# Query and key weights of differential attention, heads 2 to 7: their two float parts made during the gated MLP ahead and read back from DRAM scratch

## The chip, the cores and the metric

The kernel runs on one core of a Trainium2 chip. The metric is the time of one execution on the device in microseconds (us), lower is better. A core has five engines that run their own instruction streams and wait for one another by semaphores: PE (TensorE, matrix products), DVE (VectorE), ACT (ScalarE), POOL (GpSimd) and SP (SyncE, which here only issues DMAs). Matrix products write PSUM; all other tiles lie in SBUF; weights and scratch lie in DRAM.

## The reference, cut to what matters

A first block (a pooling mixer and block-sparse attention under a gate, then an MLP with squared ReLU) is followed by a second block whose first layer is differential attention. Sequence 512, width 1024, float32 throughout. The parts that the change touches:

```python
        u2 = rmsnorm(h, norm_mlp_pre[l])
        a = jnp.square(jax.nn.relu(u2 @ w_up[l]))          # 1024 -> 4096
        h = h + rmsnorm(a @ w_down[l], norm_mlp_post[l])   # 4096 -> 1024
...
    q, k, v = jnp.split(h @ w_qkv, 3, axis=-1)             # 1024 -> 3 x 1024
    q = apply_rope(q.reshape(B, S, 2 * H, d), cos, sin)    # H = 8, d = 64
    k = apply_rope(k.reshape(B, S, 2 * H, d), cos, sin)
    v = v.reshape(B, S, H, 2 * d)
...
        s = jnp.einsum('bqhd,bkhd->bhqk', qb, k) * scale
        pr = jax.nn.softmax(s, axis=-1).reshape(B, H, 2, DIFF_Q_BLOCK, S)
        a = (pr[:, :, 0] - lam_full * pr[:, :, 1]).astype(v.dtype)
        return jnp.einsum('bhqk,bkhe->bqhe', a, v)
...
    o = rms_norm(o, subln) * (1.0 - lam_init)
    return o.reshape(B, S, H * 2 * d) @ w_o
```

"Gated MLP" is the name of the change's own words for the MLP of the first block (`w_up`, `w_down`), the stage right ahead of differential attention.

## The kernel before, in words

Every float32 product is made of three products of rounded parts. `split` and `w_split` write a tile as hi (the rounded copy, on ACT, for every third weight tile on POOL) and lo (source minus hi, on DVE); `mm3` (L102 to L107) then issues three matmuls: hi·hi (L105), hi·lo of the activations (L106), lo·hi (L107). A weight column block of 128 outputs is a tile of 128 partitions x 1024 values (8 slices of the contraction), so its product is 8 x 3 = 24 matmuls of 512 columns.

Weights come to SBUF in tiles `wst` of 128 x 2048 values (two column blocks, 1 MB, two buffers), loaded by SP (`stage`, L99, or in `tiles`, L116, as two loads of 512 KB where the two blocks are not adjacent: query and key of one head). `w_split` makes `whi` and `wlo` of each block, four buffers each. So weights run ahead of PE by up to three split blocks and two loaded tiles.

The MLP (in `block1`) has four groups g of 8 up columns (L751 on) and 8 down columns. An up column is evacuated by DVE (`t`, L754), squared and split by ACT and DVE (L756, L79, L80); a down column is added to `y` by DVE (L778). The first three columns of each down linear are computed together (`first=3`), the rest one by one.

Differential attention (`diff`) weaves two generators. `lin` computes the linears: queries and keys of a head (`qk`), values of two heads (`vv`), in the order qk 0 and 1 together, values 0, values 1, qk 2, qk 3, qk 4, values 2, qk 5, qk 6, values 3, qk 7, then `w_o`. Each query or key goes through `rope` (copy `rx` by ACT L807, four swap DMAs `rs` on SP L811, multiplications by POOL L812 and DVE L813 and L814, split) and is then stacked by three or more DMAs on SP (`stack_q`, `stack_k`, L836 to L845). `att` walks 8 heads x 4 query tiles t: `scores` (four matmuls `sc` L852; row maximum `st` on DVE L958; exponential `pr` on ACT L961; DVE L963 to L966), two tiles later `flip` (transposes `tr` L978, split into `Th` and `Tl`), then `values` (`pv`), and the norm of a finished head. Two PSUM banks hold scores; a bank is free when ACT has read it.

The order of each engine's stream is not written out by hand: `weave` gives a program order by estimated costs, and a list scheduler places each instruction where its own clock has it ready. On the chip each engine, SP too, takes its instructions strictly in that order.

## Time and profile before

| what | value |
|---|---|
| time before, median of 3 runs | 2002.96 us (2002.18 to 2003.5) |
| time of the profiled execution | 2004.46 us |
| its span, first to last instruction | 2002.7 us |
| PE busy | 1960.4 us (98%) |
| DVE busy | 1262.8 us (63%) |
| ACT busy | 800.7 us (40%) |
| POOL busy | 444.7 us (22%) |
| DMA queue of SP | 218.19 MB, 36.8% of 16 DMA engines |

The profiled execution is 1.5 us above the median of the runs. Engine, time and wait stand in each row of the trace; an engine's gap is put down to the instruction that ended it. PE's busy time is a modelled one of pipelined matmuls, so the gaps between its instructions tell more than its share.

### The profile page before, as it was taken

To read this page: it belongs to the slowest core of one execution; us is meant where nothing else is said; L and a number is where in the kernel's file an instruction comes from. 1 tells how busy PE (TensorE), PEld (TensorE's weight loads), DVE (VectorE), ACT (ScalarE), POOL (GpSimd) and SP (SyncE) were. 2 spreads that over 40 slices of the span, in tenths; PEclk is the share of its full clock that TensorE was granted. 3 is DMA by queue.
4 is the path that set the end of the run, shared out by engine and by line. 5 is a ranking of instruction groups with operands and counts; after the bars stand their busy time and mean duration, and the time that the engine had idled before them with its cause. 6 is when DMAs were issued, how large, how long until landed. Compare 5 with 4: busy or idle time off the path is not lost.

```text
span 2002.7 us, 25458 instructions
## 1 busy us (share of the span) xinstructions
PE 1960.4 (98%) x9400; PEld 1626.0 (81%) x9400; DVE 1262.8 (63%) x2087; ACT 800.7 (40%) x1392; POOL 444.7 (22%) x545
## 2 busy tenths in 40 slices
PE   8999999999999999999999999999998999999997
PEld 7797788788888887887788888887877788888886
DVE  6447755435444478897683565658797684565665
ACT  4325434322213345554342331335575342342342
POOL 4115421000000211110221123122343221113122
PEclk9999999999999999999999999999999999999999
DMA  6263543233332446443332333336522333334231
GB/s 195 85 163 85 153 133 120 97 106 102 103 106 87 142 148 160 128 121 93 106 105 89 102 105 85 90 121 181 134 79 82 85 106 105 94 96 143 79 105 63
DMA packets 263853, 224.33 MB, mean 112 GB/s; under 512 B 9957, under 2 KB 236338, under 8 KB 263730
## 3 DMA queue, kind: packets, MB, share of 16 engines
q1 hardware_dynamic: 260538, 218.19, 36.8%
q10 hardware_dynamic: 3192, 4.52, 0.7%
q8 instruction: 74, 1.21, 0.3%
q14 instruction: 49, 0.40, 0.1%
HBM read 182.83 MB, written 14.16 MB: 98 GB/s over the span
## 4 chain that ended last, share of the span: by engine, by line
PE 50%; DVE 7%; ACT 2%; issue 2%; DMA 1%; SPq 0%; POOL 0%; DVEq 0%; ACTq 0%; POOLq 0%
PE mm L105 7%; PE mm L107 7%; PE mm L106 7%; PE sc L107 6%; PE sc L105 6%; PE sc L106 6%; PE pv L105 3%; PE pv L106 3%; PE pv L107 3%; PE sc L852 1%; DVE wlo L94 1%; PE pv L861 1%; DVE st L958 1%; DVE Tl L80 1%; DVE pr L966 1%
## 5 line engine op out<-in xcount | busy, mean ns | idle before, releaser
L94 DVE TENSOR_TENSOR wlo<-wst,whi 128x1024 fp32r<-128x1024 f32 (+2 forms) x304 | 393.6, 1298 | 198.9 <-ACT whi L93 141.0
L93 ACT ACTIVATE whi<-wst 128x1024 fp32r<-128x1024 f32 (+2 forms) x203 | 207.2, 1026 | 435.0 <-PE sc L106 171.2
L105 PE MATMUL mm<-uh,whi 128*128 128x512 f32 x712 | 281.8, 396 | 0.6 <-DVE t L754 0.6
L106 PE MATMUL mm<-ul,whi 128*128 128x512 f32 x712 | 279.3, 392 | 1.1 <-DVE ul L83 1.1
L107 PE MATMUL mm<-uh,wlo 128*128 128x512 f32 x712 | 279.1, 392 | 0.0
L91 POOL TENSOR_SCALAR whi<-wst 128x1024 fp32r<-128x1024 f32 (+2 forms) x101 | 110.6, 1095 | 756.6 <-PE mm L106 268.5
L105 PE MATMUL sc<-uh,whi 128*128 128x512 f32 x488 | 191.2, 392 | 0.0
L106 PE MATMUL sc<-ul,whi 128*128 128x512 f32 x488 | 190.7, 391 | 0.2 <-DVE ul L83 0.2
L107 PE MATMUL sc<-uh,wlo 128*128 128x512 f32 x488 | 190.7, 391 | 0.0
L107 PEld LDWEIGHTS mm<-uh,wlo 128*128 128x128 f32 x712 | 134.3, 189 | 27.4
L106 PEld LDWEIGHTS mm<-ul,whi 128*128 128x128 f32 x712 | 134.4, 189 | 26.8 <-DVE ul L83 1.6
L105 PEld LDWEIGHTS mm<-uh,whi 128*128 128x128 f32 x712 | 134.5, 189 | 26.4 <-DVE t L754 0.8
L107 PEld LDWEIGHTS sc<-uh,wlo 128*128 128x128 f32 x488 | 91.9, 188 | 20.2 <-DVE wlo L94 0.7
L106 PEld LDWEIGHTS sc<-ul,whi 128*128 128x128 f32 x488 | 91.9, 188 | 19.1 <-DVE ul L83 0.5
L105 PEld LDWEIGHTS sc<-uh,whi 128*128 128x128 f32 x488 | 91.9, 188 | 18.7
L105 PE MATMUL sc<-ah,whi 128*128 128x512 f32 x264 | 102.8, 389 | 0.0
L107 PE MATMUL sc<-ah,wlo 128*128 128x512 f32 x264 | 102.7, 389 | 0.0
L106 PE MATMUL sc<-al,whi 128*128 128x512 f32 x264 | 102.7, 389 | 0.0
L105 PE MATMUL pv<-uh,whi 128*128 128x512 f32 x256 | 100.4, 392 | 1.0 <-DVE psl L83 1.0
L107 PE MATMUL pv<-uh,wlo 128*128 128x512 f32 x256 | 99.8, 390 | 0.0
L106 PE MATMUL pv<-ul,whi 128*128 128x512 f32 x256 | 99.8, 390 | 0.0
L1263 ACT ACTIVATE cv<-cu,cc 128x512 f32<-128x512 f32 x88 | 70.9, 813 | 60.2 <-DVE cu L1261 59.3
(460 smaller groups left out, 4307.4 us busy)
## 6 DMA issues: line engine op xcount, KB each, us to landing
wst<-ffn_w_up SPq DMA_DIRECT2D x88, 512.0 KB
wst<-w_up SPq DMA_DIRECT2D x16, 1024.0 KB
wst<-w_down SPq DMA_DIRECT2D x16, 1024.0 KB
wst<-ffn_w_down SPq DMA_DIRECT2D x16, 1024.0 KB
wst<-w_in SPq DMA_DIRECT2D x16, 512.0 KB
wst<-w_in SPq DMA_DIRECT2D x8, 1024.0 KB
wst<-diff_w_qkv SPq DMA_DIRECT2D x16, 512.0 KB
wst<-ple_w_gate SPq DMA_DIRECT2D x8, 1024.0 KB
```

The source lines that it names most:

```text
L80: nc.vector.tensor_tensor(lo, src, f32(hi), op=OP.subtract)
L91: nc.gpsimd.tensor_scalar(hi, src, 1.0, 1.0, op0=OP.mult, op1=OP.mult)
L93: nc.scalar.activation(hi, src, AF.Copy)
L94: nc.vector.tensor_tensor(lo, src, f32(hi), op=OP.subtract)
L105: nc.tensor.matmul(ps, ah, bh, start=first, stop=False)
L106: nc.tensor.matmul(ps, ah, bl, start=False, stop=False)
L107: nc.tensor.matmul(ps, al, bh, start=False, stop=last)
L852: self.nc.tensor.matmul(ps, q[m][:, qs], k[2 * step + m][:, ks], start=step == 0, stop=last and step == 1)
L861: nc.tensor.matmul(*args, start=first and x == 0, stop=last and x == 1)
L958: nc.vector.reduce_max(st[:, m:m + 1], ps, axis=AX.X, negate=True)
L966: nc.vector.scalar_tensor_tensor(pr[0], pr[1], st[:, 6:7], pr[0], op0=OP.mult, op1=OP.add)
L1263: nc.scalar.activation(v, u[:, 1:S + 1], AF.Identity, bias=cc[:, 3, ft:ft + 1], scale=cc[:, 1, ft:ft + 1])
```

## The change

`presplit` is a generator that takes 24 jobs: head 2 to 7, query or key, lower or upper half of the contraction. A job loads a half block `xs` (128 x 512 values, 256 KB) on SP, makes hi on ACT and lo on DVE (both tiles are called `xh` in the rows), and stores both (2 x 256 KB) on SP into DRAM scratch `xd0h`, `xd0l` to `xd11h`, `xd11l`. All three SBUF tiles have one buffer. One job is asked for after each evacuated column: 8 down columns of g = 1, 8 up columns and 8 down columns of g = 2. Later, `split_load` reads a block's parts from the scratch straight into `whi` and `wlo` (2 x 512 KB on SP) for qk 2 to 7, in place of the load to `wst` and the split.

```diff
@@ -93,6 +94,43 @@
+    def presplit(self, w, jobs, P, bufs):
+        nc = self.nc
+        src = w.rearrange("(k p) n -> p k n", p=128)
+        done = None
+        for key, k0, kt, cols in jobs:
+            n = 128 // len(cols)
+            st = P.tile([128, kt, 128], F32, name="xs", tag="xs", bufs=bufs)
+            for i, c in enumerate(cols):
+                nc.sync.dma_start(st[:, :, i * n:(i + 1) * n], src[:, k0:k0 + kt, c:c + n])
+            pair = [P.tile([128, kt, 128], F32R, name="xh", tag=t, bufs=bufs) for t in ("xh", "xl")]
+            nc.scalar.activation(pair[0], st, AF.Copy)
+            nc.vector.tensor_tensor(pair[1], st, f32(pair[0]), op=OP.subtract)
+            if bufs == 1:
+                self.split_store(key, k0, pair)
+            else:
...
+            yield
...
+    def split_store(self, key, k0, pair):
+        if key not in self.pres:
+            self.pres[key] = [self.dr.tile([128, KT, 128], F32, name="xd%d%s" % (len(self.pres), "hl"[i]))
+                              for i in range(2)]
+        for d, t in zip(self.pres[key], pair):
+            self.nc.sync.dma_start(d[:, k0:k0 + t.shape[1], :], f32(t))
+
+    def split_load(self, key):
+        wt = [self.wp.tile([128, KT, 128], F32R, name=t, tag=t, bufs=4) for t in ("whi", "wlo")]
+        for t, d in zip(wt, self.pres[key]):
+            self.nc.sync.dma_start(f32(t), d)
+        return wt
@@ -121,14 +159,14 @@
-        src = self.tiles(w, k0, kt, cols[len(ahead):])
+        src = (self.split_load(key) for key in pres) if pres else self.tiles(w, k0, kt, cols[len(ahead):])
@@ -758,6 +796,8 @@
                     at.append((hi, lo))
+                    if g >= 2:
+                        next(X, None)
@@ -768,6 +808,11 @@
+                if g == 1:
+                    X = self.presplit(a["diff_w_qkv_2"][0],
+                                      [(("d", h, n), k0, 4, [1024 * n + h * 128]) for h in range(2, KT)
+                                       for n in range(2) for k0 in (0, 4)],
+                                      cv.enter_context(tc.tile_pool(name="pre", bufs=1)), 1)
@@ -776,6 +821,8 @@
+                    if g in (1, 2):
+                        next(X, None)
@@ -784,6 +831,8 @@
+            assert next(X, None) is None
+            cv.close()
@@ -935,7 +984,7 @@
                 return self.linear_steps(w, self.u, [h * 128, 1024 + h * 128], evac,
-                                         hold=("dqkfree", h - 2) if h >= 2 else None)
+                                         hold=("dqkfree", h - 2), pres=[("d", h, 0), ("d", h, 1)])
```

What the scheduler makes of it is seen at three places of the streams. (The changed kernel's line numbers are higher: its L108 and L127 are the jobs' loads and stores, L110 and L111 their hi and lo, L132 the loads from scratch; L137, L143 to L145, L901 and L1027 are L99, L105 to L107, L852 and L978 of before.)

The first is SP's stream in the MLP, from the first up tile of g = 2 on; `xs` is a job's half block, `xd` the scratch, `wst` the MLP's weights. Before, the weight loads stand there alone:

```order
L99 DMA wst<-w_up 128x8x256 x4
L99 DMA wst<-w_down 128x8x256 x4
L99 DMA wst<-w_up 128x8x256 x4
```

The changed kernel has:

```order
L137 DMA wst_4562<-w_up 128x8x256
L108 DMA xs_4338<-diff_w_qkv_2 128x4x128
L137 DMA wst_4572<-w_up 128x8x256
L127 DMA xd0h_4344<-xh_4340 128x512
L127 DMA xd0l_4345<-xh_4341 128x512
L108 DMA xs_4349<-diff_w_qkv_2 128x4x128
L127 DMA xd0h_4344<-xh_4351 128x512
L127 DMA xd0l_4345<-xh_4352 128x512
L108 DMA xs_4358<-diff_w_qkv_2 128x4x128
L137 DMA wst_4666<-w_up 128x8x256
L127 DMA xd1h_4364<-xh_4360 128x512
L127 DMA xd1l_4365<-xh_4361 128x512
```

Between two weight tiles there are now two jobs, six DMAs, and each weight load stands between a job's load and its stores.

The second is ACT's stream at the start of the down linear of g = 2 in the changed kernel; `s` and `ah` are of the last up column, `whi` the split of weight blocks. Of these rows the stream of before has only those on `s`, `ah` and `whi`, in the same order.

```order
L794 ACTIVATE s_4924<-t_4922 128x512
L80 ACTIVATE ah_4926<-s_4924 128x512
L110 ACTIVATE xh_4801<-xs_4799 128x512
L110 ACTIVATE xh_4848<-xs_4846 128x512
L110 ACTIVATE xh_4889<-xs_4887 128x512
L94 ACTIVATE whi_5066<-wst_5064 128x1024
L94 ACTIVATE whi_5070<-wst_5064 128x1024
```

Jobs 12, 13 and 14 (counted from 0) stand in front of the splits of two weight blocks.

The third is the begin of the scores in differential attention, on PE and on SP. Before, PE has finished the query of head 2 (`pv`, 24 matmuls) when the scores of head 0 (`sc`) begin, and goes on with its key (`mm`) between them:

```order
L106 MATMUL pv_6371<-ul7_5811,whi_6363 128x512
L107 MATMUL pv_6371<-uh7_5810,wlo_6364 128x512
L852 MATMUL sc_6398<-st2_6060,st0_6010 128x512
L852 MATMUL sc_6399<-st3_6061,st1_6011 128x512
L852 MATMUL sc_6398<-dl1_6062,st0_6010 128x512
L852 MATMUL sc_6399<-dm_6075,st1_6011 128x512
L105 MATMUL mm_6488<-uh0_5796,whi_6367 128x512
L106 MATMUL mm_6488<-ul0_5797,whi_6367 128x512
```

In the changed kernel the first two matmuls of head 2's query are followed by fourteen score matmuls and a flip (`tr`), of which the last rows are shown, and only then comes the first matmul that reads `wlo`:

```order
L1027 MATMUL tr_6664<-ident_72,pr0_6622 128x128 x4
L901 MATMUL sc_6648<-st3_6281,st1_6231 128x512
L901 MATMUL sc_6648<-dm_6295,st1_6231 128x512
L901 MATMUL sc_6672<-st2_6280,st0_6230 128x512
L901 MATMUL sc_6672<-dl1_6282,st0_6230 128x512
L145 MATMUL pv_6588<-uh0_6016,wlo_6581 128x512
L143 MATMUL pv_6588<-uh1_6018,whi_6580 128x512
```

On SP of the changed kernel the load of that `wlo` (`xd0l`) stands behind the stacking of heads 0 and 1 (`st`, `dm`, `dl`) and the swaps of head 1's key (`rs`), while that of its `whi` stands ahead of them:

```order
L132 DMA whi_6580<-xd0h_4344 128x1024
L892 DMA st3_6281<-st2_6280 64x512
L893 DMA st3_6281<-st2_6280 64x512
L892 DMA dm_6295<-dl1_6282 64x512
L893 DMA dm_6295<-dl1_6282 64x512
L885 DMA st5_6303<-st4_6302 64x512
L894 DMA st2_6280<-st2_6280 64x512
L886 DMA st5_6303<-dl0_6304 64x512
L894 DMA dl1_6282<-dl1_6282 64x512
L887 DMA st4_6302<-dl0_6304 64x512
L860 DMA rs_6325<-rx_6323 32x512 x4
L132 DMA wlo_6581<-xd0l_4345 128x1024
```

So the two parts of one weight block are now issued eleven rows apart, and the matmul that needs the second waits behind the scores of four query tiles.

## Rows read from the trace of the kernel before

**Rows 1.** The page: its span, and each engine's busy us, share of the span and instructions.

```profile
span 2002.7 us, 25458 instructions
PE 1960.4 (98%) x9400; PEld 1626.0 (81%) x9400; DVE 1262.8 (63%) x2087; ACT 800.7 (40%) x1392; POOL 444.7 (22%) x545
```

**Rows 2.** Busy time by stretch: the stretch in us, its length, busy us of PE, PEld, DVE, ACT, POOL (instructions), granted clock of PE (1.00 is 2.4 GHz), share of the DMA engines, GB/s. The first lies in the MLP, the second in differential attention.

```profile
540.00:590.00 50.00, 50.00 (x222) 41.42 (x221) 21.32 (x24) 11.44 (x15) 3.17 (x3) 1.00 0.33 105
750.00:800.00 50.00, 47.12 (x243) 38.30 (x242) 43.83 (x77) 28.47 (x59) 8.72 (x6) 1.00 0.63 159
```

**Rows 3.** Waits of PE from 740 to 955 us: who waited for whom, us in total, times, longest.

```profile
PE sc L852 <- ACT pr L961: 5.0, 6, 2.3
```

**Rows 4.** Groups of instructions from 740 to 960 us: line, engine, operation, tiles, shapes, count, then busy us and mean ns of one, then the idle time before them and its releasers.

```profile
L94 DVE TENSOR_TENSOR wlo<-wst,whi 128x1024 fp32r<-128x1024 f32 x23 | 30.2, 1312 | 6.3 <-ACT whi L93 3.8 <-POOL whi L91 2.4
L93 ACT ACTIVATE whi<-wst 128x1024 fp32r<-128x1024 f32 x16 | 16.8, 1058 | 5.8 <-PE mm L106 2.4 <-PE pv L107 1.8 <-PE sc L106 1.6
L961 ACT ACTIVATE pr<-sc,st 128x512 f32<-128x512 f32 x64 | 43.9, 690 | 27.9 <-DVE st L958 27.6
L961 ACT ACTIVATION_READ_ACCUMULATOR pr<-sc,st 128x1 f32 x64 | 12.7, 199 | 0.0
L958 DVE TENSOR_REDUCE st<-sc 128x1 f32<-128x512 f32 x64 | 43.1, 681 | 5.7 <-PE sc L852 5.7
```

**Rows 5.** Timeline of PE: start us, us, engine, line, operation, tiles, shapes, count, and in brackets the idle time before it and what ended it.

```profile
752.08 0.40 PE L105 MATMUL pv<-uh,whi 128*128 128x512 f32 x1
...
757.55 0.62 PE L852 MATMUL sc<-st,st 128*128 128x512 f32 x2
...
763.15 0.49 PE L852 MATMUL sc<-st,st 128*128 128x512 f32 x1 [0.23 <-ACT pr L961]
...
768.22 0.50 PE L852 MATMUL sc<-st,st 128*128 128x512 f32 x1 [2.26 <-ACT pr L961]
...
778.83 0.38 PE L106 MATMUL pv<-Tl,V 128*128 128x256 f32 x1 [0.39 <-DVE Tl L80]
...
803.36 0.50 PE L852 MATMUL sc<-st,st 128*128 128x512 f32 x1 [1.25 <-ACT pr L961]
```

**Rows 6.** Timelines of DVE and POOL ahead of the longest of these waits (768.22), columns as in rows 5.

```profile
763.70 2.31 DVE L94 TENSOR_TENSOR wlo<-wst,whi 128x1024 fp32r<-128x1024 f32 x1 [1.35 <-POOL whi L91]
766.67 0.68 DVE L958 TENSOR_REDUCE st<-sc 128x1 f32<-128x512 f32 x1
762.62 1.05 POOL L91 TENSOR_SCALAR whi<-wst 128x1024 fp32r<-128x1024 f32 x1 [1.66 <-DMA wst<-diff_w_qkv]
```

**Rows 7.** The chain of work that ended last: start us, us, what. The transfer is one of 512 KB, with four swaps of 64 KB issued beside it.

```profile
757.62 4.83 DMA wst<-diff_w_qkv
```

**Rows 8.** Timelines of POOL and SP around the rope of heads 0 and 1, columns as in rows 5; an SP row is a DMA's issue.

```profile
743.28 1.68 POOL L91 TENSOR_SCALAR whi<-wst 128x1024 fp32r<-128x1024 f32 x1 [6.10 <-ACT whi L93]
744.92 2.98 POOL L812 TENSOR_TENSOR rs<-rs,R 128x512 f32<-128x512 f32 x2
749.14 0.50 SPq L843 DMA_DIRECT2D st<-st  x1
757.62 0.58 SPq L116 DMA_DIRECT2D wst<-diff_w_qkv  x1
```

**Rows 9.** Timeline of DVE in the MLP: evacuations of two neighbouring up columns of g = 2, of its first down columns, the weight split ahead of the place of job 0, and a split of half a block's size.

```profile
497.45 1.21 DVE L94 TENSOR_TENSOR wlo<-wst,whi 128x1024 fp32r<-128x1024 f32 x1
522.00 0.69 DVE L754 SCALAR_TENSOR_TENSOR t<-mm,R 128x512 f32<-128x512 f32 x1 [3.35 <-PE mm L107]
524.06 0.69 DVE L80 TENSOR_TENSOR al<-s,ah 128x512 fp32r<-128x512 f32 x1
527.44 0.69 DVE L754 SCALAR_TENSOR_TENSOR t<-sc,R 128x512 f32<-128x512 f32 x1 [2.69 <-PE sc L107]
575.04 0.69 DVE L778 TENSOR_TENSOR y<-mm,y 128x512 f32<-128x512 f32 x1 [12.16 <-PE mm L107]
```

**Rows 10.** Timelines in the MLP: ACT's half-size split and its two weight splits at the start of the down linear of g = 2, and PE's first matmul with the block that they make.

```profile
561.47 0.63 ACT L79 ACTIVATE ah<-s 128x512 fp32r<-128x512 f32 x1
574.86 2.01 ACT L93 ACTIVATE whi<-wst 128x1024 fp32r<-128x1024 f32 x2 [12.76 <-PE mm L106]
581.64 0.39 PE L105 MATMUL pv<-ah,whi 128*128 128x512 f32 x1
```

**Rows 11.** Issues on SP in the MLP: two weight loads of 1 MB, one after the other.

```profile
507.80 0.37 SPq L99 DMA_DIRECT2D wst<-w_up  x1
518.73 0.37 SPq L99 DMA_DIRECT2D wst<-w_up  x1
```

**Rows 12.** A load of 1 MB by stretch, with no other transfer beside it (columns as in rows 2).

```profile
404.00:405.00 1.00, 1.00 (x6) 0.84 (x5) 0.98 (x1) 0.00 (x0) 0.00 (x0) 1.00 0.02 7
404.00:409.00 5.00, 5.00 (x24) 4.14 (x23) 2.20 (x2) 1.54 (x2) 0.00 (x0) 1.00 0.67 210
```

**Rows 13.** A store of 256 KB to DRAM scratch, issued by ACT, and the DVE instruction that waited for its landing (columns as in rows 5).

```profile
486.00 0.33 ACTq L288 DMA_DIRECT2D sin<-red  x1
488.14 1.34 DVE L283 SCALAR_TENSOR_TENSOR red<-kk,ang 128x512 f32<-128x512 f32 x1 [2.14 <-DMA sin<-red]
```

**Rows 14.** Two stretches in which PE was granted less than its full clock (columns as in rows 2).

```profile
365.00:370.00 5.00, 3.94 (x14) 2.95 (x14) 4.40 (x9) 4.16 (x7) 0.00 (x0) 0.77 0.51 163
370.00:375.00 5.00, 5.00 (x21) 4.04 (x21) 3.63 (x7) 3.19 (x6) 0.00 (x0) 0.89 0.00 0
```

More of the change, by code (lines that the diff above doesn't have):

```diff
@@ L48, in __init__ @@
         self.pjd = []
+        self.pres = {}
         self.consts()
@@ L95, in w_split @@
         return hi, lo
+    def presplit(self, w, jobs, P, bufs):
[13 more added lines that the diff above has]
+            else:
+                if done:
+                    self.split_store(*done)
+                done = key, k0, pair
+            yield
+        if done:
+            self.split_store(*done)
+    def split_store(self, key, k0, pair):
[9 more added lines that the diff above has]
+        return wt
     def stage(self, w, k0, kt, c0, nc_):
@@ L123, in linear_steps @@
     def linear_steps(self, w, x, cols, evac, k0=0, group=1, order=None, ready=None, first=None, ahead=(), hold=None,
-                     mid=None):
+                     mid=None, pres=None):
         kt = len(x)
```

## The prediction

> **What bounds the kernel now.** The page comes first: PE is busy 98% of the span and the next engine, DVE, 63% [rows 1]. So the kernel ends when PE has done its matmuls, and what a change of the other engines' work can give is no more than the time in which PE waits for them. The busy times by stretch say where that is: in the MLP PE is busy 50.00 of 50 us with DVE at 21 and ACT at 11, so there is room on both engines and nothing to gain; at the start of differential attention PE loses 2.9 of 50 us while DVE is busy 43.8 [rows 2]. There DVE is the near bound. The list of PE's waits names the chain: 5.0 us in six waits, scores that wait for the exponential that frees their PSUM bank [rows 3]; the timeline of PE adds 0.39 us for a split of transposed probabilities [rows 5]. These 5.4 us are all that the change can win in attention. Two of the waits stand close together at 763.15 and 768.22, 0.23 + 2.26 = 2.5 us [rows 5]. Their cause is one weight split: POOL's half of it waited for the load, DVE then waited 1.35 us for POOL and took 2.31 us, and the row maximum of the scores stood behind it until 766.67 [rows 6]. The load had taken 4.8 us [rows 7].
>
> **What is removed.** Twelve of the 23 weight splits of the attention stretch (six heads, query and key): on DVE 12 x 1.31 = 15.7 us of 200, and on ACT or POOL 12 copies of about 1.06 us [rows 4]. PE's matmuls stay. DVE's 43.8 of 50 us becomes about 40, so waits for its queue should shrink. The wait of 2.26 us is of the removed kind as to its cause, but its place is taken by another (below). Two more waits with row maxima or splits late in DVE's queue, 0.39 at 778.83 and 1.25 at 803.36 [rows 5], I count as won: -1.6 us. Bounds: nothing (the queue refills), and -5.4 us (all seven).
>
> **What is added in the MLP.** 24 jobs of one ACT copy of 0.63 us and one DVE subtraction of 0.69 us (the same operations at this size) [rows 9, 10]: 0.6 and 0.7 us beside each column of 5.44 us (522.00 to 527.44) [rows 9]. The cover is the idle time of ACT and DVE there [rows 2]; were it gone, all 24 would cost 24 x 1.3 = 32 us. What matters is their chain, since there is one buffer: load, copy, subtraction, two stores, next load. No row shows the 256 KB load. From below it is the 2.14 us from issue to landing of a 256 KB store (486.00 to 488.14) [rows 13]; from above the 4.83 us of 512 KB among other transfers [rows 7]. With 0.63 + 0.69 and two further issues of about 0.55 us each on SP (0.50 and 0.58) [rows 8], a job takes 2.14 + 1.32 + 1.1 = 4.6 to 4.83 + 1.32 + 1.1 = 7.3 us. Against the columns that is 5.44 us, and the streams tie two jobs to one weight load, which is released every 10.93 us (507.80 to 518.73) [rows 11], so jobs can't run ahead of the columns. Can the transfers keep up? A pair of jobs and a weight tile move 2 x 0.79 + 1.05 = 2.62 MB; 1 MB alone moved at (210 x 5 - 7) / 4 = 261 GB/s [rows 12]; that is 10.0 us of 10.93. Tight, but it fits, so I take 5.44 us a job, near the lower end, since the rate row bears it out.
>
> The place where lateness would reach PE is the start of the down linear of g = 2, where jobs 12 to 14 stand ahead of ACT's next weight splits. Job 0 stands behind the split that ends at 498.7 [rows 9], so it is done at 499.4, and job 14 at 499.4 + 14 x 5.44 = 575.6. Behind it on ACT are the two splits that started at 574.86 [rows 10]; behind it on DVE three evacuations (3 x 0.69 us, from 575.04) [rows 9] and the lo part, 1.2 us: ready at 578.9. PE reads the block at 581.64 [rows 10]. So 2.7 us of slack, and a job may take 5.44 + 2.7 / 14 = 5.6 us at no cost. Elsewhere three weight blocks are ready ahead, 3 x 5.44 = 16 us less a split. Cost taken: 0. Upper bound, at 7.3 us a job: 14 x 1.7 = 24 us.
>
> **A rule against it.** The 2.14 us of the store row [rows 13] is of the MLP, where the DMA engines' share was 0.33 [rows 2]. The Trainium skill, "DMA: Bandwidth & Descriptors", section "Latency and other measured facts", says that the access to HBM, 0.2 us on average, takes 2 us at high load, and that this makes up most of a DMA's fixed cost. By that figure, as an estimate, a job would take 4.6 + 1.8 = 6.4 us and the MLP would cost 14 x 0.8 = 11 us; by the row it costs nothing. No row here shows a queue as full as this one will be.
>
> **What moves in attention.** The parts of heads 2 to 7 are no longer loaded ahead to a spare tile and then split; they are loaded straight to `whi` and `wlo`, so the load can only start when these are free, and stands in SP's queue among swaps and stackings. The order shows what that does to head 2: PE has two matmuls of its query, then must do fourteen score matmuls and a flip, then the first matmul with `wlo`. Before, PE began that query at 752.08 and had 24 matmuls (to 757.55) to fill the time [rows 5]. Now three rounds of scores stand there, each released by the last: row maximum 0.68, exponential 0.69, its sum 0.20, two score matmuls 0.45, together 2.0, with the semaphores 2.15 us [rows 4, 5]. From the two matmuls' end, 752.5, first scores to 753.4, three rounds 6.5, last scores 0.45: about 760.4. Of these 7.9 us PE works 14 x 0.23 = 3.2 (the flip adds little), so it idles 4.7 us. Will the first scores be ready at 752.5? They were stacked from 749.14 on; POOL did a weight split first and took the key's swap at 744.92 [rows 8]; without it, and without two DVE splits, the chain starts some 2 to 4 us earlier, so yes. Is `wlo` there by 760.4? Its load stands where 757.62 stood [rows 8] or up to 4 us earlier; with 4.83 us [rows 7] it lands between 758.5 and 762.4; I take the scores as the later one. Cost: 4.7 less the 2.5 that stood here, +2.2 us; from below 0 (the scores run quicker), from above 762.4 - 752.5 - 3.2 - 2.5 = +4.2 us.
>
> For heads 3 to 7 the load is issued behind the swaps of the query two places ahead, at least one 24-matmul column (5.44 us) and its share of attention before use; a load is 2.1 to 4.8 us. I cost these at nothing; behind a late one stand the swaps of the next rope, wanted only for scores four tiles later. From above: 2 us for one in two of ten blocks, 10 us in all, which would need the queue to be full throughout.
>
> **Sum.** -1.6 + 0 + 2.2 + 0 = +0.6 us, against a profiled time of 2004.46 us (span 2002.7), 1.5 above the median of the runs; on the median 2002.96 that is 2003.6 us. A change of 0.2%, 4 us, is about what a measurement tells from none.
>
> **The rivals.** (1) No change, within 4 us: what the sum says. It is also the case that the change does not do what it seems made for: DVE's relief comes where PE didn't wait. Chance 0.52.
> (2) Faster: the loads land early, the scheduler's waiting order costs no more than before, and the lighter DVE frees every score bank in time: -5.4, 1997.6 us. For it: the waits in rows 3 are all at the far end of DVE's queue. Against: the fourteen scores in a row can't go faster than their banks. It decides once the first place idles under 1.5 us. Chance 0.15.
> (3) Slower, by the chain of jobs: at 6.4 us a job, job 14 ends at 589 and PE waits 14 x 0.8 = 11 us, 2014 us. From 5.9 us a job on it is over 4 us. For it: 10.0 of 10.93 us of transfers, one buffer, stores and weights in one queue. Against: 2.14 us a store. This is where the skill's rule on load would lead. Chance 0.18.
> (4) Slower, in attention: `wlo` of head 2 late, +4.2, the other waits not won, 0, and the clock. PE was granted 0.77 and 0.89 of its clock in two stretches of 5 us after short waits, at the lower of its levels for part of it (1.2 instead of 2.4 GHz), which is 5 x 0.23 + 5 x 0.11 = 1.7 us lost [rows 14]; beside the wait of 2.26 us it kept 1.00 [rows 2]. A wait of over 4 us may bring it: +5.9, 2008.9 us. Chance 0.15.
>
> **The range.** Case 1 spans 1999 to 2007. Down to 1998 takes in most of case 2, up to 2010 case 4 and the milder third of case 3; what is left out is about 2 in 10. Faster 0.15, same 0.52, slower 0.33. I predict 2003.6 us.
>
> **What would show it.** The wait ahead of the first matmul of head 2's query that reads `wlo`: about 4.7 us in all and ended by the score bank if I am right, by the load in case 4. The busy times by stretch in the MLP: PE 50.00 of 50 still, DMA share 0.7 to 0.9; a gap of PE near 581 would be case 3, with job 14's subtraction after 578. DVE in 750 to 800: about 40. The waits at 778 and 803 gone. I am wrong if PE waits at several heads for `whi` or `wlo`, or if ACT's copies in the MLP end waits for `xs` of several us each.

## The result: slower, and mostly where the prediction had put a zero

The changed kernel takes 2024.51 us (median of 4 runs, 2022.83 to 2028.11) against 2002.93 us; the ratio is 1.0114, 95% interval 1.0102 to 1.0126. The forecast was 2003.6 us with a range from 1998 to 2010. The span and the engines on the page of the changed kernel, beside [rows 1]:

```profile
span 2022.9 us, 25656 instructions
PE 1969.8 (97%) x9400; PEld 1629.9 (81%) x9400; DVE 1262.4 (62%) x2099; ACT 807.6 (40%) x1408; POOL 437.1 (22%) x541
```

DVE does no more work than before, PE's matmuls are the same 9400, and the span is 20.2 us longer. Where it goes is read by setting four events of both traces side by side: the start on PE of the down column of g = 1 during which the first job is loaded (494.60 before, 495.20 now), the first value matmul that waited for `rx` (739.98 and 756.84), the last flip (938.65 and 960.43), and the end. The distance grows from 0.6 to 16.9 us in the MLP, to 21.8 us in attention, and is 20.2 us at the end. So the MLP costs 16.3 us, attention 4.9 us, and the stretch behind gives 1.6 us back. In the runs below (but for e5, whose edit reaches that far) what lies behind the linear after attention takes between 0.1 us more and 3.1 us less than before, though no edit touches it; so the 1.6 us say nothing of the change.

Busy time by stretch of the changed kernel, columns as in [rows 2]:

```profile
520.00:570.00 50.00, 44.92 (x191) 35.82 (x190) 25.38 (x31) 19.60 (x28) 3.31 (x3) 0.96 0.63 202
570.00:620.00 50.00, 46.15 (x186) 37.19 (x185) 20.36 (x25) 11.06 (x15) 2.11 (x2) 0.90 0.67 215
```

PE, which was busy 50.00 of 50 us there, now loses 5.1 and 3.9 us, and its granted clock falls. DMA stands at 0.63 and 0.67. The timeline of PE has the waits (columns as in [rows 5]):

```profile
561.84 0.50 PE L143 MATMUL sc<-ah,whi 128*128 128x512 f32 x1 [0.52 <-ACT whi L94]
563.94 0.50 PE L145 MATMUL sc<-ah,wlo 128*128 128x512 f32 x1 [1.37 <-DVE wlo L95]
567.35 0.80 PE L143 MATMUL mm<-ah,whi 128*128 128x512 f32 x1 [2.91 <-ACT whi L94]
569.45 0.63 PE L143 MATMUL mm<-ah,whi 128*128 128x512 f32 x1
...
593.00 0.50 PE L143 MATMUL pv<-ah,whi 128*128 128x512 f32 x1 [1.88 <-ACT whi L94]
595.70 0.80 PE L145 MATMUL pv<-ah,wlo 128*128 128x512 f32 x1 [1.97 <-DVE wlo L95]
```

All wait for a weight split. After 567 a matmul stands at 0.63 instead of 0.39 us: the clock is at the lower of its two levels. Two stretches of 5 us show how far:

```profile
570.00:575.00 5.00, 5.00 (x17) 3.96 (x16) 0.81 (x2) 0.63 (x1) 0.00 (x0) 0.68 0.27 89
595.00:600.00 5.00, 4.30 (x10) 3.44 (x11) 4.98 (x6) 1.58 (x2) 0.00 (x0) 0.50 0.53 132
```

Summed over such stretches from 560 to 605, idle time is 8.9 us, and busy time times the part of the clock not granted is 5.1 us. With a wait of 0.5 us at 666 that is 14.5 of the 16.3 us.

Why the splits are late stands on ACT and SP. ACT at the first place and at the second (timeline):

```profile
560.20 0.63 ACT L110 ACTIVATE xh<-xs 128x512 fp32r<-128x512 f32 x1 [4.67 <-DMA xs<-diff_w_qkv]
560.74 1.05 ACT L94 ACTIVATE whi<-wst 128x1024 fp32r<-128x1024 f32 x1
...
586.36 0.63 ACT L110 ACTIVATE xh<-xs 128x512 fp32r<-128x512 f32 x1 [7.32 <-DMA xs<-diff_w_qkv]
591.37 0.63 ACT L110 ACTIVATE xh<-xs 128x512 fp32r<-128x512 f32 x1 [4.38 <-DMA xs<-diff_w_qkv]
591.90 1.99 ACT L94 ACTIVATE whi<-wst 128x1024 fp32r<-128x1024 f32 x2
```

The first copy is job 9's, and the split behind it is the one that PE waits for at 561.84. The last two copies are of jobs 13 and 14; behind them stand the two splits that were made at 574.86 before [rows 10], and PE waits for the first of them at 593.00. And SP, one weight tile and the jobs around it:

```profile
549.01 0.39 SPq L108 DMA_DIRECT2D xs<-diff_w_qkv  x1
550.33 0.38 SPq L137 DMA_DIRECT2D wst<-w_down  x1
552.90 0.34 SPq L127 DMA_DIRECT2D xd4h<-xh  x1
553.63 0.34 SPq L127 DMA_DIRECT2D xd4l<-xh  x1
554.06 0.61 SPq L108 DMA_DIRECT2D xs<-diff_w_qkv  x1
560.86 0.32 SPq L127 DMA_DIRECT2D xd4h<-xh  x1
...
562.59 0.39 SPq L108 DMA_DIRECT2D xs<-diff_w_qkv  x1
563.96 0.38 SPq L137 DMA_DIRECT2D wst<-w_down  x1
```

The load at 549.01 was ready for ACT 3.2 us later (552.24), the one at 554.06 only after 6.1 us (560.20): the second is issued behind a weight tile of 1 MB and two stores. The trace has sixteen landings for each transfer, one for each of its parts. The last parts of that weight tile, of the two stores and of the load come one behind the other, at 558.05, 558.73, 559.37 and 560.12: the load waits its turn. And it waits for few parts: twelve of its sixteen are there by 557.72, the last four between 559.29 and 560.12, while the DMA engines are already falling idle (columns as in [rows 2]):

```profile
556.00:557.00 1.00, 1.00 (x6) 0.84 (x5) 0.25 (x1) 0.00 (x0) 0.00 (x0) 1.00 0.87 269
558.00:559.00 1.00, 1.00 (x6) 0.84 (x5) 0.00 (x0) 0.00 (x0) 0.00 (x0) 1.00 0.26 91
559.00:560.00 1.00, 1.00 (x6) 0.83 (x5) 0.00 (x0) 0.00 (x0) 0.00 (x0) 1.00 0.11 32
```

In the five long loads of jobs 5 to 14 the last four parts come 1.4 to 2.8 us behind the twelfth, in the five short ones 0.2 to 0.4. That is some 2 of the 3.1 us by which a long load exceeds a short one. In the kernel before, the last four parts of a weight tile come 0.1 to 0.5 us behind the twelfth. Why four parts are late in the change is not shown.

Load, copy, subtraction, two issues, twice: 549.01 to 562.59 is 13.6 us for two jobs, and the weight tile between them comes 13.6 us after the last (550.33, 563.96). The columns want one every 10.9 us [rows 11].

### The profile page after: what moved, and what is told of

Read it like the earlier page. It is cut to its first block, busy times and chain, and to the rows that moved or that the text cites. A ratio compares the mean times of both kernels' runs of the same rounds, so it can differ in the third digit from the quotient of the medians.

```text
span 2022.9 us, 25656 instructions
## 1 busy us (share of the span) xinstructions
PE 1969.8 (97%) x9400; PEld 1629.9 (81%) x9400; DVE 1262.4 (62%) x2099; ACT 807.6 (40%) x1408; POOL 437.1 (22%) x541
## 4 chain that ended last, share of the span: by engine, by line
PE 73%; DVE 10%; DMA 8%; ACT 4%; issue 3%; POOL 1%; SPq 1%; ACTq 0%; DVEq 0%; POOLq 0%
PE mm L145 10%; PE mm L143 10%; PE mm L144 10%; PE sc L144 9%; PE sc L145 9%; PE sc L143 9%; DMA xs<-diff_w_qkv 5%; PE pv L143 4%; PE pv L145 4%; PE pv L144 4%; PE sc L901 2%; DVE wlo L95 1%; PE pv L910 1%; DVE xh L111 1%; ACT xh L110 1%
## 5 line engine op out<-in xcount | busy, mean ns | idle before, releaser
L95 DVE TENSOR_TENSOR wlo<-wst,whi 128x1024 fp32r<-128x1024 f32 (+2 forms) x292 | 378.2, 1299 | 194.6 <-ACT whi L94 138.6
L94 ACT ACTIVATE whi<-wst 128x1024 fp32r<-128x1024 f32 (+2 forms) x195 | 198.4, 1023 | 349.2 <-PE sc L144 138.1
L143 PE MATMUL mm<-uh,whi 128*128 128x512 f32 x712 | 282.1, 396 | 0.7 <-DVE t L792 0.6
L145 PE MATMUL mm<-uh,wlo 128*128 128x512 f32 x712 | 279.5, 393 | 0.0
L143 PE MATMUL sc<-uh,whi 128*128 128x512 f32 x488 | 191.3, 392 | 0.0
L145 PE MATMUL sc<-uh,wlo 128*128 128x512 f32 x488 | 190.8, 391 | 0.0
L145 PEld LDWEIGHTS mm<-uh,wlo 128*128 128x128 f32 x712 | 134.3, 189 | 27.6 <-DMA wlo<-xd3l 0.2
L143 PEld LDWEIGHTS mm<-uh,whi 128*128 128x128 f32 x712 | 134.6, 189 | 26.8 <-DVE t L792 0.8
L145 PEld LDWEIGHTS sc<-uh,wlo 128*128 128x128 f32 x488 | 91.9, 188 | 20.1 <-DVE wlo L95 0.7
L143 PEld LDWEIGHTS sc<-uh,whi 128*128 128x128 f32 x488 | 91.9, 188 | 18.8
L145 PE MATMUL sc<-ah,wlo 128*128 128x512 f32 x264 | 103.2, 391 | 1.9 <-DVE wlo L95 1.9
L143 PE MATMUL sc<-ah,whi 128*128 128x512 f32 x264 | 103.2, 391 | 0.5 <-ACT whi L94 0.5
L143 PE MATMUL pv<-uh,whi 128*128 128x512 f32 x256 | 100.7, 393 | 1.0 <-DVE psl L84 1.0
L145 PE MATMUL pv<-uh,wlo 128*128 128x512 f32 x256 | 100.2, 391 | 0.0
L143 PE MATMUL mm<-ah,whi 128*128 128x512 f32 x236 | 92.7, 393 | 2.9 <-ACT whi L94 2.9
```

Source lines behind the costliest of these rows:

```text
L94: nc.scalar.activation(hi, src, AF.Copy)
L95: nc.vector.tensor_tensor(lo, src, f32(hi), op=OP.subtract)
L143: nc.tensor.matmul(ps, ah, bh, start=first, stop=False)
L145: nc.tensor.matmul(ps, al, bh, start=False, stop=last)
```

## The experiments

The table sets each run against the profiled kernel before: MLP from PE's start of the column at 494.60 to the value linear, attention from there to the last flip, then the output linear up to its last matmul; "job" is the mean distance of the jobs' copies. Runs whose attention is that of before differ from it by up to 0.6 us there: that is the error of the attention column. The times of the whole take in the stretches ahead and behind as well.

| run | median us | ratio (95%) | MLP | attention | output linear | job |
|---|---|---|---|---|---|---|
| change | 2024.51 | 1.0114 (1.0102 to 1.0126) | +16.3 | +4.9 | 0.0 | 6.3 |
| e1_jobs_only | 2019.30 | 1.0075 (1.0060 to 1.0090) | +13.5 | -0.1 | 0.0 | 6.1 |
| e2_scratch_only | 2005.11 | 1.0013 (1.0004 to 1.0023) | 0.0 | +2.1 | 0.0 | - |
| e3_load_ahead | 2020.73 | 1.0086 (1.0071 to 1.0101) | +14.8 | +3.3 | 0.0 | 4.9 |
| e4_spread | 2009.00 | 1.0032 (1.0021 to 1.0042) | +3.3 | +2.9 | 0.0 | 8.6 |
| e5_heads3to7 | 2008.97 | 1.0034 (1.0022 to 1.0045) | 0.0 | -0.6 | +3.1 | 8.3 |
| e6_no_stores | 2001.92 | 0.9996 (0.9986 to 1.0005) | 0.0 | -0.4 | 0.0 | 5.3 |
| e7_pool_split | 2022.73 | 1.0102 (1.0086 to 1.0118) | +21.0 | +0.1 | 0.0 | 6.5 |
| e8_pool_all | 2028.41 | 1.0127 (1.0111 to 1.0143) | +25.1 | +3.0 | +0.4 | 8.5 |
| e9_phase | 1999.25 | 0.9987 (0.9978 to 0.9996) | 0.0 | -0.8 | 0.0 | 8.3 |
| e10_pool_dma | 2024.68 | 1.0110 (1.0095 to 1.0124) | +23.8 | -0.4 | +0.4 | 6.5 |
| e11_pool_loads | 2019.35 | 1.0088 (1.0074 to 1.0103) | +1.1 | +15.1 | 0.0 | 7.0 |
| e12_ahead_tied | 2007.89 | 1.0025 (1.0015 to 1.0034) | +5.1 | -0.6 | 0.0 | 5.1 |

### The two halves apart

```diff
# e1_jobs_only
-hold=("dqkfree", h - 2), pres=[("d", h, 0), ("d", h, 1)])
+hold=("dqkfree", h - 2) if h >= 2 else None)
```

> The 24 jobs in the MLP as in the change, but heads 2 to 7 of attention load and split their weights as the kernel before does; the scratch is written and never read. In the changed kernel the first matmul of the value linear came 16.9 us later than before. Theory (chain of jobs late, ACT's and DVE's weight splits behind them): that loss stays whole, 2018 to 2022 us, PE idle about 9 us in the two places of the MLP and granted less than its clock behind them. Rival (the jobs cost little by themselves, the loss comes with the reading of the scratch): within 4 us of before.

```diff
# e2_scratch_only
-for h in range(2, KT) for n in range(2) for k0 in (0, 4)]
+for h in range(2, 3) for n in range(1) for k0 in (0, 4)]
...
-pres=[("d", h, 0), ("d", h, 1)]
+pres=[("d", 2, 0)] * 2
```

> Attention as in the change, with the MLP left almost alone: only two jobs are done, and all twelve blocks of heads 2 to 7 load the one pair of scratch tiles that they fill (so the weights of these heads are those of one block). Theory: the attention stretch alone loses what it lost in the changed kernel, from the first value matmul to the last flip 4.9 us, so 2006 to 2009 us. Rival (attention loses only because the MLP's late jobs or stores reach into it): within 2 us of before, or faster, since DVE is relieved of twelve splits.

The jobs alone cost 16.8 us of median, the scratch alone 2.6 us. The loss belongs to the jobs; attention has a smaller one of its own, +2.1 us here, where the clock stayed at 1.00, and +4.9 us in the change, where it did not. Of e2 the theory had asked for 4.9 us and 2006 us or more, the rival for a time within 2 us of before: the result lies between the two. The rest of the 4.9 us came only with the jobs in place, the lower clock among it.

### Pace, bytes, or order

```diff
# e3_load_ahead: xs has two buffers, a job's load is issued before the job ahead of it is worked on
+ahead = []
+for x, (key, k0, kt, cols) in enumerate(jobs):
+    while len(ahead) < 2 and x + len(ahead) < len(jobs):
+        _, q0, _, c = jobs[x + len(ahead)]
+        st = P.tile([128, kt, 128], F32, name="xs", tag="xs", bufs=2)
+        nc.sync.dma_start(st, src[:, q0:q0 + kt, c[0]:c[0] + 128])
+        ahead.append(st)
+    st = ahead.pop(0)
```

> The change with two buffers for the half block xs, the load of a job issued ahead of the stores of the job before. Theory A (the chain through one buffer sets the pace: 3.2 or 6.5 us of load, copy, subtraction, two issues, next load): the chain loses the copy, subtraction and issues from its loop, a pair takes 11 us or less in place of 13.6, and the MLP costs under 5 us: 2006 to 2012 us. Theory B (transfers are the bound, the queue is as full as it gets): the pair stays at 13 us or more and the time within 4 us of the change, 2020 to 2026 us.

A miss: a job takes 4.9 us, as theory A wanted, and the time stays, as theory B wanted. The orders can explain it without a full queue (the DMA share was 0.79 from 520 to 570). On SP, jobs depend on no column, so the scheduler sets them as early as the buffers allow, two and three in turn to a weight tile. 2.5 jobs of 4.9 us are 12.3 us to a tile; the first six tiles came 13.0 us apart on average, as in the change (13.0), where the columns want 10.9. On ACT, `xh` still has one buffer, so a copy now waits for the landing of the store ahead, and the splits stand behind it as before (timeline; PE then waits 5.34 us at 591.49):

```profile
585.54 0.63 ACT L113 ACTIVATE xh<-xs 128x512 fp32r<-128x512 f32 x1 [7.91 <-DMA xd8h<-xh]
590.39 1.99 ACT L94 ACTIVATE whi<-wst 128x1024 fp32r<-128x1024 f32 x2
```

```diff
# e4_spread: 24 jobs for 40 columns; the load waits for its column
+if seen[0] * 24 // 40 != (seen[0] - 1) * 24 // 40:
+    self.tie = f32(t) if t.dtype == F32R else t
+    next(X, None)
...
+nc.vector.tensor_copy(st[:, 0, 0:1], self.tie[:, 0:1])
 nc.sync.dma_start(st[:, :, i * n:(i + 1) * n], src[:, k0:k0 + kt, c:c + n])
```

> The 24 jobs spread over 40 columns (down of g = 1, up and down of g = 2 and 3), three jobs to five columns, each load made to wait for its column by a one-element DVE copy into xs. One buffer as in the change. Theory (a job takes 6.8 us on average and only its pace against the columns matters): a job every 9.1 us keeps up, PE does not wait in the MLP, and the time is that of attention's loss alone, 2006 to 2009 us. Rival (each job delays the splits behind it whatever the pace): waits of PE of 0.5 us or more stay at several places in the MLP, above 2012 us.

No wait of PE at any column; what is left is one of 2.2 us for the squares' sum at the end, beside the last jobs. At 8.6 us a job the MLP keeps up, with the same 24 jobs, and the time is at the upper end of the theory's range.

```diff
# e6_no_stores: tied to each of the 24 columns, attention as before
-self.split_store(key, k0, pair)
+pass
```

> Jobs of load, copy and subtraction alone, one buffer, each load tied to its column; the stores are left out and attention splits its weights as before. Theory (it is the serial chain against the columns): with the store issues (1.1 us a job) and half a megabyte a job out of the queue, a job takes under 5.4 us, PE does not wait in the MLP, and the time is within 3 us of before. Rival (any job's copy ahead of a weight split costs, whatever its length): waits of PE in the MLP of some us stay, 2010 us or more.

Held: a job every 5.3 us, one per column, and PE waits nowhere in the MLP. Here a copy ahead of a split costs nothing while the chain keeps the beat.

```diff
# e12_ahead_tied: e3's loop, the load tied to each column as in e4, attention as before
+nc.vector.tensor_copy(st[:, 0, 0:1], self.tie[:, 0:1])
 nc.sync.dma_start(st, src[:, q0:q0 + kt, c[0]:c[0] + 128])
```

> The jobs alone (attention as before), with two buffers of xs and the load issued a job ahead, and each load tied to its column (one job per column of 5.44 us, as the change means it). In the run with two buffers and no tie a job took 4.9 us on average, but jobs ran ahead of the columns, two or three between two weight tiles, and the tiles came 12.5 us apart where the columns want 10.9. Theory (what PE loses is decided by jobs between two weight tiles times the time of a job, not by the bytes): with two jobs to a tile and 4.9 to 5.4 us a job the tiles keep their 10.9 us, and the time is within 4 us of before, 2000 to 2007 us. Rival (the queue's bytes are the limit: 24 jobs in 24 columns can't be carried): PE loses 8 us or more in the MLP, 2011 us or more.

Between the two: 5.6 us of median, one wait of 2.4 and one of 0.5 us instead of the many. The scheduler still set 16 jobs to seven tiles, 2.3 x 5.1 = 11.7 us to a tile, and the first six tiles came 11.9 us apart on average. (In e3 it was 13.0, not the 12.5 of the expectation.) That fits the order, but the DMA share was 0.80 here, and this run does not tell whether 24 jobs in 24 columns could be carried at all.

### Which shared order carries the lateness

```diff
# e7_pool_split: attention as before; w_split makes no split on POOL in g = 1 and 2
-nc.scalar.activation(pair[0], st, AF.Copy)
-nc.vector.tensor_tensor(pair[1], st, f32(pair[0]), op=OP.subtract)
+nc.gpsimd.tensor_scalar(pair[0], st, 1.0, 1.0, op0=OP.mult, op1=OP.mult)
+nc.gpsimd.tensor_tensor(pair[1], st, f32(pair[0]), op=OP.subtract)
```

> As the run with the jobs alone (attention as before), but a job's copy and subtraction are done by POOL, which in the two groups concerned makes no weight splits (ACT makes them all). Loads and stores stay on SP among the weight tiles, and a job's chain gets no shorter. Theory A (weight splits are late because they stand behind jobs in ACT's and DVE's order): the loss of the MLP falls under 4 us, 2003 to 2007 us. Theory B (weight tiles are late because their loads stand behind a job's stores in SP's order, 13.6 us apart where the columns want 10.9): the loss stays or grows, 2018 us or more.

The loss stays: SP's order alone is enough, for the split that ends the first wait stands behind no job and waits for its weight tile (ACT's row below). But the first wait comes only at 607.17, 45 us later than in the change, so ACT's and DVE's orders had brought the early ones:

```profile
607.17 0.80 PE L144 MATMUL sc<-uh,whi 128*128 128x512 f32 x1 [3.81 <-ACT whi L95]
...
606.06 2.00 ACT L95 ACTIVATE whi<-wst 128x1024 fp32r<-128x1024 f32 x2 [23.19 <-DMA wst<-w_up]
```

```diff
# e10_pool_dma: attention as before; no splits on POOL from g = 1 on
-nc.sync.dma_start(st[:, :, i * n:(i + 1) * n], src[:, k0:k0 + kt, c:c + n])
+nc.gpsimd.dma_start(st[:, :, i * n:(i + 1) * n], src[:, k0:k0 + kt, c:c + n])
...
-self.nc.sync.dma_start(d[:, k0:k0 + t.shape[1], :], f32(t))
+self.nc.gpsimd.dma_start(d[:, k0:k0 + t.shape[1], :], f32(t))
```

> The jobs alone (attention as before), with only their loads and stores moved from SP to POOL's queue; copy and subtraction stay on ACT and DVE, POOL makes no weight splits from g = 1 on. SP's order holds weight tiles alone. Theory (either order that jobs share with the weights passes their lateness on): ACT's and DVE's splits still stand behind late jobs, PE waits 5 us or more in the MLP, 2010 to 2024 us. Rival (SP's order is the only carrier): no waits of PE there, 2001 to 2005 us.

Held, with a time 0.7 us above the range named: with SP free of jobs, ACT's and DVE's orders alone are enough too. PE waits from 561.42 on, and a wait of 3.81 us ends with a split behind a late copy:

```profile
562.91 0.63 ACT L111 ACTIVATE xh<-xs 128x512 fp32r<-128x512 f32 x1 [3.06 <-DMA xs<-diff_w_qkv]
564.63 1.04 ACT L95 ACTIVATE whi<-wst 128x1024 fp32r<-128x1024 f32 x1
565.72 0.79 PE L144 MATMUL mm<-ah,whi 128*128 128x512 f32 x1 [3.81 <-ACT whi L95]
```

```diff
# e8_pool_all: e7's and e10's edits together, attention as in the change
```

> The change with the whole job on POOL, its load and its stores issued from there too, and no weight splits on POOL from g = 1 on. SP, ACT and DVE hold nothing of the jobs. Under A as under B the MLP then costs nothing and the time is attention's loss alone, 2005 to 2010 us. Rival C (the DMA engines are so full that the weight tiles come late wherever the jobs are issued): PE still waits some 5 to 10 us in the MLP, 2012 us or more.

The time is the worst of all, where rival C had it, and yet this run speaks against rival C. Busy time by stretch:

```profile
520.00:570.00 50.00, 50.00 (x222) 41.41 (x221) 21.90 (x24) 17.75 (x24) 22.10 (x28) 1.00 0.59 187
570.00:620.00 50.00, 50.00 (x222) 41.40 (x221) 23.98 (x24) 14.62 (x17) 22.32 (x28) 1.00 0.61 195
...
680.00:700.00 20.00, 0.00 (x0) 0.00 (x0) 0.00 (x0) 1.10 (x2) 12.02 (x16) 0.59 0.31 105
```

Ahead of 680 us the DMA share and rate are nearly those of the change (0.63 and 0.67, 202 and 215 GB/s), and PE waits nowhere. So at some 190 GB/s the bytes alone make no column wait. The 21.56 us come behind the columns: at 8.5 us a job the last one on POOL ends at 697, and POOL's sum of squares for the norm, on which ACT and then PE wait, stands behind it:

```profile
697.60 1.27 POOL L384 TENSOR_TENSOR acc<-acc,sq 128x512 f32<-128x512 f32 x1
698.90 0.63 ACT L382 ACTIVATE sq<-y 128x512 f32<-128x512 f32 x1 [33.52 <-POOL acc L384]
700.53 0.79 PE L144 MATMUL mm<-ah,whi 128*128 128x512 f32 x1 [21.56 <-ACT whi L95]
```

### Attention

```diff
# e5_heads3to7: 20 jobs tied to 20 of 32 columns, head 2 as before
-for h in range(2, KT)
+for h in range(3, KT)
...
-pres=[("d", h, 0), ("d", h, 1)]
+pres=[("d", h, 0), ("d", h, 1)] if h >= 3 else None
```

> Twenty jobs for heads 3 to 7, tied to 20 of the 32 columns from the down linear of g = 1 to the up linear of g = 3; head 2 is loaded and split as before. Theory (what is left of the loss at 24 spread jobs is the 2.2 us at the end of the MLP, where jobs stood beside the last columns, and some 3 us in attention around the first scores, where head 2's second part comes late): both go, PE idles 2.5 us around 763 to 769 as before, and the time is 2000 to 2005 us. Rival (loads of parts cost attention at every head): 2006 us or more with waits for whi or wlo at several heads.

Half a hit: the MLP costs nothing and attention nothing (0.0, -0.6), so the loss in attention is head 2's. The time is in the rival's range, though not by the rival's cause. The linear behind attention lost 3.1 us, in two waits that neither theory had:

```profile
PE mm L146 <- DVE wlo L95: 2.6, 1, 2.6
PE sc L146 <- DVE wlo L95: 1.3, 1, 1.3
```

```diff
# e9_phase: e5 and one line in split_load
+self.turn += 1
 wt = [self.wp.tile([128, KT, 128], F32R, name=t, tag=t, bufs=4) for t in ("whi", "wlo")]
```

> The twenty spread jobs for heads 3 to 7 with one edit more: a block read from scratch counts as a split in the counter that sends every third split to POOL, so that the splits of the linear behind attention fall on the same engines as in the kernel before. In the run with heads 3 to 7 attention took 0.6 us less than before up to the last flip, and the linear behind it 3.1 us more, with two waits for lo parts of 1.32 and 2.56 us. Theory (these two waits come of the ten missing counts, which move splits of that linear to POOL): they go, and the time is within 2.5 us of before, 2001 to 2005.5 us. Rival (they come of late loads or of a fuller DVE): they stay, 2006 to 2010 us.

The cause held, the size did not (the time is below the range named): both waits go. `w_split` sends every third split to POOL by a counter; ten splits fewer shift it, the change's twelve do not. This is the fastest kernel of the study, 1999.25 us, 0.9987 (0.9978 to 0.9996). But of the fourteen executions of the kernel before that it is set against, three took 1998.98 to 1999.29 us too. Its waits in attention beside the 5.0 us of [rows 3]:

```profile
PE sc L911 <- ACT pr L1020: 2.2, 5, 0.8
PE tr L1037 <- DVE pr L1025: 1.7, 2, 1.2
```

The pattern changes, and the sum is 3.9 instead of 5.4 us. Of the 5.3 us by which its profiled span is shorter, only 0.8 lie in stretches that the edits touch (0.0 in the MLP, -0.8 in attention); 1.4 lie ahead of them and 3.1 behind. Where its gain comes from is open, and whether it is one.

```diff
# e11_pool_loads: 24 jobs tied to 24 of 32 columns
 for t, d in zip(wt, self.pres[key]):
-    self.nc.sync.dma_start(f32(t), d)
+    self.nc.gpsimd.dma_start(f32(t), d)
```

> All 24 jobs, tied to three columns in four (32 columns, one job per 7.3 us), and attention's loads from scratch issued by POOL in place of SP. In PE's order the scores of head 0 then stand between the matmuls of head 2 as in the kernel before, not fourteen in a row. Theory (attention's loss is the place of head 2's second load behind swaps and stackings, 2.7 to 4.9 us with the lower clock): from the first value matmul after the last rope copy to the last flip it takes 198 to 199 us (198.7 before, 203.6 in the change), and with an MLP that keeps up the time is 2001 to 2005 us. Rival (the loads as such hinder attention's stackings and swaps, whoever issues them): 200.5 us or more there, 2005 us or more in all.

The MLP keeps up at 7.0 us a job. Attention does not win but loses 15.1 us: POOL issued nine loads of 512 KB between 742 and 759 us, the DMA share rose to 0.88, and the stackings of the first scores came late. The numbers are those of the rival; they fit that early loads issued by another engine hinder the rope, and do not say that the place of head 2's load was harmless. The row below has 5.3 of the 15.1 us with a clock of 0.86 beside it; PE waits at ten more places up to 932.64, by up to 2.6 us, and those were not traced back.

Busy time by stretch, and PE's wait:

```profile
745.00:770.00 25.00, 19.70 (x104) 16.59 (x103) 7.79 (x14) 5.33 (x11) 7.53 (x11) 0.86 0.88 251
```

```profile
762.48 1.19 PE L910 MATMUL sc<-st,st 128*128 128x512 f32 x2 [4.52 <-DMA st<-st]
```

## Why the prediction was wrong, step by step

**The bound, and what can be won.** Right. PE is still the bound, and relief of DVE won little: attention with ten splits fewer is 0.8 us shorter at best (e9), where -1.6 was taken; runs with the attention of before differ from it by up to 0.6.

**A job at 5.44 us, cost taken 0.** This is the step that failed. The prediction had both ends, 4.6 and 7.3 us, and went near the lower one on the ground that the bytes fit: 10.0 of 10.93 us. But a job is a chain through one buffer, and its pace is the sum of its latencies, not its bytes. From job 0 to job 14 it took (591.37 - 501.61) / 14 = 6.41 us. The term that was mis-sized is the load. From job 1 to job 14 it took 4.6 us on average (from job 5 on 3.1 to 3.3 and 6.0 to 6.7 us in turn), near the 4.83 us of the upper bound and not the 2.14 of the lower; the rest of the chain took 1.8 us where 2.4 had been set. That the bytes fit is shown at the rate that was reached (e8, e9: 187 to 201 GB/s, no wait at a column). At the rate forecast, 2.62 MB in 10.93 us or 240 GB/s, it is not shown: e3 and e12 came to 241 and 246 GB/s in one stretch each, and lost 14.8 and 5.1 us.

**The cover.** "Elsewhere three weight blocks are ready ahead", 16 us, was taken for good everywhere but at one place. Each weight load stands on SP between a job's load and its stores, as the order showed, and the loads of the change were issued 12.3, 12.4, 13.6 and 13.6 us apart (498.47 to 550.33) in place of 10.9: 8.1 us late by 550. The splits stood behind late copies on ACT besides, the one at 560.74 behind job 9's. The first wait came at 561.84, some twenty us ahead of the place that the prediction watched. How much of the cover each order took is not shown; without jobs on ACT and DVE the first wait came 45 us later (e7).

**Rival 3** named the mechanism and the pace, 6.4 us a job, and had 0.18. Its sign came too: job 14's subtraction at 592.03, after 578, and PE's gap at 593.00 for the block that it read at 581.64 before. Its price, 11 us, was too low for 16.3: PE waits in the up columns already, 5.1 us, and each place is followed by some us at the lower clock, 5.1 us in all, which the prediction had priced (1.7 us) in attention alone. The rule of the Trainium skill ("DMA: Bandwidth & Descriptors", section "Latency and other measured facts") gave 6.4 us a job, and 6.41 was measured. The trace does not show its reason, though. By the rule's figure, as an estimate, a load would take 2.14 + 1.8 = 3.9 us. Measured were 4.6, and the shorter rest of the chain (1.8 for 2.4 us) made up for it, so the agreement is luck. Equal loads took about 3.2 or about 6.3 us by what had been issued just ahead of them, nothing as large or a weight tile and two stores, and landed behind these. That is a queue, and not a latency that grew for all.

**The first scores in attention.** The place was right, and for the greater part the releaser; the size was too small. PE and SP of the changed kernel:

```profile
769.16 0.40 PE L144 MATMUL pv<-ul,whi 128*128 128x512 f32 x1
770.56 0.71 PE L901 MATMUL sc<-st,st 128*128 128x512 f32 x2 [1.00 <-DMA st<-st]
771.68 0.49 PE L901 MATMUL sc<-dl,st 128*128 128x512 f32 x1 [0.17 <-DMA dl<-dl]
773.10 0.50 PE L901 MATMUL sc<-st,st 128*128 128x512 f32 x1 [0.93 <-ACT pr L1010]
775.42 0.79 PE L901 MATMUL sc<-st,st 128*128 128x512 f32 x1 [0.93 <-ACT pr L1010]
777.98 0.80 PE L901 MATMUL sc<-st,st 128*128 128x512 f32 x1 [0.30 <-ACT pr L1010]
779.86 0.63 PE L145 MATMUL pv<-uh,wlo 128*128 128x512 f32 x1
```

The `wlo` load was issued on SP at 773.13, and the clock in the last five us was at its lower level:

```profile
773.13 0.58 SPq L132 DMA_DIRECT2D wlo<-xd0l  x1
```

```profile
775.00:780.00 5.00, 4.28 (x11) 2.81 (x12) 4.97 (x9) 2.94 (x8) 0.97 (x1) 0.50 0.76 282
```

From the end of the two matmuls (about 769.4) to the first matmul with `wlo` it took 10.5 us where 7.9 were forecast. Two things were missing: the first scores were not ready ("so yes" was wrong, 1.2 us until the stackings landed), and the clock at 0.50 took 4.28 x 0.50 = 2.1 us. PE idled less than forecast, 3.3 us and not 4.7. The other 2.2 us of idling were ended by the score banks, as forecast, and not by the load. In the rest of attention no wait for `whi` or `wlo` appears in the change, as forecast (e4 has one, 0.52 us, for a part of head 3). So the 2.6 us that were too few here and the 1.6 us that were not won (below) make up 4.2 of the 4.3 us by which attention missed its +0.6. The sum there, +4.9 us, is near rival 4's +5.9 by luck: 4.2 of that was for a late `wlo`, which did not come.

**Signs named ahead.** DMA share in the MLP: 0.63 to 0.67, not 0.7 to 0.9. DVE in the 50 us after the first scores: 36.4 us busy, not 40. The waits at 778 and 803 are gone, but others came (0.15, 0.34, 0.56, 1.03, 0.38 us), so their 1.6 us were not won. The sign for being wrong, ACT waiting for `xs`, is there at every job (1.6 to 8.7 us).

**What stays open.** Whether 24 jobs in 24 columns could be carried with a better order (e12 lost 5.1 us at a DMA share of 0.80), why the last four parts of a load behind a weight tile came late, and why e9's untouched stretches were 4.5 us shorter in its profiled execution.

## What to carry to other kernels

Work put into idle engines beside a busy one is to be priced as a chain: latency of load, operations, stores and issues, in the state of the queue that it will meet, times the jobs that stand between two instructions of the main stream; free bytes and free engine time did not tell it here. In engines that take instructions strictly in order, a late side job delays the main work behind it by way of each order that it shares: SP's alone was enough (e7), ACT's and DVE's alone (e10), and in the end POOL's (e8). Work ready ahead hides this only until it is used up, so the first wait can lie far ahead of the place where the jobs look dangerous. A side job without a dependence on the main work is set by this scheduler as early as its buffers allow: to be paced, it has to depend on what paces it (e4, e6), and one dependence may not be enough: e12, tied to each column, still had three jobs to some weight tiles.

## What had not been expected of the hardware

A wait can cost more than its length: after idle times of 1.4 to 2.9 us PE ran at 1.2 GHz for some us, 5.1 us of lost work beside 8.9 us of idling, while the wait of 2.26 us in the kernel before left it at 1.00 [rows 2]. A load of 256 KB took twice as long (6.3 for 3.2 us) when a weight tile and two stores had been issued in the 4 us ahead of it, and some 2 of the 3 us between them were the last four of its sixteen parts. And the count of splits sent round two engines matters beyond the stretch that is changed: ten splits fewer moved others to POOL, 3.1 us in the linear behind, which one line took back.
